# Expert stage: matmuls in program order, background work spread over the experts, a gather moved ahead of a branch

## The chip, the cores and the metric

One core of a Trainium2 chip runs the kernel. The time is device microseconds, the median of three runs. A profile of one further execution shows the engines: TensorE (PE, and PEld for its weight loads), VectorE (DVE), ScalarE (ACT), GpSimd (POOL) and SyncE (SP), which here issues the weight loads. Each engine works through its own queue in order and waits for others at semaphores.

## The reference, cut to what matters

Two transformer blocks on one sequence of 256 tokens, model width 1024, float32. The first block mixes by convolution and windowed attention and ends in a mixture of 32 experts. The second mixes by attention with an extra context and by a long ("Hyena") convolution, and ends in a PEER layer. The change lies in the experts of the first block:

```python
order = jnp.argsort(expert_id, stable=True)          # two experts per token
...
hmid = jax.nn.silu(xb @ w_gate[e]) * (xb @ w_up[e])  # 1024 -> 512
return (hmid @ w_down[e]) * wt[:, None]              # 512 -> 1024
...
out = jnp.zeros((t, d)).at[slot_token].add(ys)
h = h + hierarchical_moe(rms_norm(h, g_ffn[l]), ...)
```

Beside them the kernel computes things of the second block that don't depend on the first: keys and values of the context (`context_kv`) and the spectra of the two Hyena filters (`implicit_filters`: three sine layers, a fourth matmul, a decay, a division by the sum of absolute values, a Fourier transform).

## The kernel before, in words

Each expert gets 64 slots. `gather` (L957 on) builds, for four experts at a time, the one-hot selection on VectorE and multiplies it with the tokens on TensorE (L977, L978); the result `XT` holds the inputs of the four experts. Then per expert: `expert_up` multiplies with gate and up weights, the two in different halves of the array's columns, into one PSUM tile (L1013), and ScalarE copies it to `ex` (L1016); `expert_mid` transposes it (L1024) and forms the gated product `em` on ScalarE and VectorE (L1026 to L1029); `expert_down` multiplies with the down weights (L1041), again in two column halves, and ScalarE and VectorE scale by the slot's weight into `eyh`, `eyl` (L1047, L1048). Every two experts, `selw` transposes their selection weights (L995) and `combine` multiplies back to tokens (L1059) and adds to `h` (L1061). A float32 matmul shows as two instructions.

The weights come as tiles of 512 KB, eight for up and four for down per expert, on SyncE's queue (`wload`, L87), into a ring of 14 tiles. Sixteen more buffers serve once, at the stage's start, for experts 1 and 2 (`early`); `self.wrap` is set until they are used up, and until then no background runs, since it needs their space. A load waits until the tile's last reader is done.

The loop is `experts(lo, hi)` (L846 on). It traces down of the expert before behind up of this one. The background is a Python generator, `background` (L1064 on); each `yield` ends a step, there are 33, and `back()` runs one, twice per expert. The generator's own loads are issued by ScalarE.

The order of the trace isn't the order of issue. The framework's scheduler plans all engines with a cost model: among instructions that are ready it takes the one traced first, so it may set matmuls of other parts into a run where its model has the next weights late. `add_manual_dep` with NoSync fixes the order of two instructions on one engine, without a semaphore.

After 28 experts comes `overflow`, a block under a runtime condition (more than 64 tokens for some expert) on all engines; nothing crosses it. The first eight tiles of expert 28 (`pre`) are loaded ahead of it. It isn't taken with these inputs: no instruction of it is in the trace. Then `experts(28, 32, pre)` runs the last four.

Of the kernel before, what the change touches and what calls it, by code (L numbers as in the profile page):

```python
# [8 lines left out]
F32 = mybir.dt.float32  # L9
F32R = mybir.dt.float32r  # L10
# [3 lines left out]
AF = mybir.ActivationFunctionType  # L14
OP = mybir.AluOpType
# [4 lines left out]
D = 1024  # L20
# [24 lines left out]
class K:  # L45
# [693 lines left out]
    def moe(self):  # L739
# [105 lines left out]

        def experts(lo, hi, pre=None):  # L846
            def group(e):
                return self.gather(R[:, :, e:e + 4], W[:, :, e:e + 4])

            cur = group(lo)  # L850
            sws, mid, pend, y = [], None, None, None
            for e in range(lo, hi + 1):

                if e < hi:
                    if e % 4 == 0 and e > lo:
                        cur = nxt
# [15 lines left out]
                if e > lo and e % 2 == 0:  # L872
                    pend = y, sws.pop(0)
            self.combine(*pend)

        bg = None

        def back():
            nonlocal bg
            if not self.wrap:  # L880
                if not bg:
                    self.open_bp()
                    bg = self.background()
                next(bg, 0)

# [4 lines left out]
        self.wrap = pools  # L890
        experts(0, 28)
        for _ in bg:
# [11 lines left out]
        nc.vector.tensor_tensor(self.gf2, self.gf, self.gf, op=OP.mult)  # L904
        experts(28, 32, pre)

    def overflow(self, many, wg, wu, wd):
# [3 lines left out]
        with self.tc.If(many > 64):  # L911
# [12 lines left out]
            for j in range(7):  # L924
# [22 lines left out]
                e = nc.values_load(ei[0:1, 0:1], engines=[mybir.EngineType.SP], min_val=0, max_val=31)  # L947
                XT, sw = self.gather(rj, wj)

# [8 lines left out]

    def gather(self, R4, W4):
# [5 lines left out]
        sg = self.T(me, [128, 2, 4, 64], F32R, "selg", 2)[:, :, 0:n, :]  # L965
        tt(sg, self.iota[:, None, None, 0:64].to_broadcast(sh), R4[:, :, :, None].to_broadcast(sh), op=OP.is_equal)
        sw = self.T(me, [128, 2, 4, 64], F32, "selw", 2)[:, :, 0:n, :]
        tt(sw, sg.bitcast(F32), W4[:, :, :, None].to_broadcast(sh), op=OP.mult)
        XT = self.T(me, [128, 8, 256], F32, "XT", 2)[:, :, 0:64 * n]
# [12 lines left out]
        return XT, sw  # L982

# [48 lines left out]
    def expert_down(self, m, d, odd, sw, y=None):  # L1032
# [30 lines left out]

    def background(self):  # L1064
        nc, A, l1, hp = self.nc, self.A, self.l2, self.hp
        bp = self.bp
# [5 lines left out]
        for t in range(2):  # L1072
# [10 lines left out]
        yield  # L1083
        hc = []
        for k2 in range(4):
# [11 lines left out]
            yield  # L1097
        kc = self.T(bp, [128, 2, 128], F32, "sa", 1)
        for i in range(2):
# [8 lines left out]
            nc.scalar.activation(o, p[:, :S].rearrange("p (t c) -> p t c", t=2), AF.Copy)  # L1108
            yield
        sq = self.T(bp, [128, 2, 128], F32, "sn", 1)  # L1110
# [7 lines left out]
        tt(k4, k4, self.rv[:, None, o:o + 64].to_broadcast([128, 4, 64]), op=OP.mult)  # L1118
        yield
# [4 lines left out]
        yield  # L1124

# [6 lines left out]
        for i in range(3):  # L1132
# [13 lines left out]
            if i < 2:  # L1146
                w = wf[:, 64 * (i + 1):64 * (i + 2)]
            yield
        dec = self.T(bp, [128, 2, 512], F32, "dec")
# [7 lines left out]
        for o in range(2):  # L1157
            rsk = self.T(hp, [128, 2, 512], F32, "lo")
            rn, sk = rsk[:, 0], rsk[:, 1]
            nc.scalar.dma_start(sk, A["skip"][o:o + 1, :].to_broadcast([128, 512]))  # L1160
            pn = self.ps()
            fb = []
            w4 = self.T(hp, [64, 2, 512], F32, "hi")
            nc.scalar.dma_start(w4, A["hfw4"][:, 1024 * o:1024 * o + 1024].rearrange("p (a c) -> p a c", a=2))
            for dr in range(2):
                f = self.T(hp, [128, 2, 512], F32, "hi")
                for t in range(2):
                    p = self.ps()
                    nc.tensor.matmul(p, cur[:, t * 128:(t + 1) * 128], w4[:, dr, :], start=True, stop=True)
                    tt(f[:, t, :], p, dec[:, t, :], op=OP.mult)  # L1170
                    if dr == 1 and t == 0:

                        nc.vector.memset(f[0:1, 0, :], 0.0)
# [3 lines left out]
                    yield  # L1177
# [6 lines left out]
            tt(df, fb[0], fb[1], op=OP.subtract)  # L1184
            yield
            kf = [self.T(l1, [128, 2, 512], F32, "kf%s%d" % (c, o)) for c in "ab"]
            kf = [kf[i // 2][:, i % 2, :] if i < 4 else kfc[:, o] for i in range(5)]
            for i in range(5):
# [6 lines left out]
                if i not in (2, 3):  # L1195
                    tt(kf[i], kf[i], sk, op=OP.add)
                yield
            self.kf.append(kf)
# [931 lines left out]
```

## Time and profile before

| | |
|---|---|
| median of 3 runs | 1667.43 us (1666.98 to 1669.1) |
| the profiled execution | 1665.63 us |
| its span, first to last instruction | 1663.8 us |
| PE busy | 1573.6 us (95%) |
| DVE busy | 965.0 us (58%) |
| ACT busy | 495.3 us (30%) |
| moved by DMA | 536.53 MB |
| granted PE clock, mean | 0.981 |

The expert stage reaches from about 200 to 745 us of the span. A busy PE isn't a PE at its peak: the ends of matmuls are modelled, so short pauses between shapes don't show as idle. The distance from one start to the next tells more than a duration does. "Granted clock" is the share of 2.4 GHz that the chip let PE have.

### The profile page before, as it was taken

The numbers are of one execution on the slowest core, as the hardware profiler recorded it, in microseconds if no ns is written. First come the engines' busy times: TensorE is split into PE (matmuls) and PEld (weight loads), VectorE is DVE, ScalarE is ACT, GpSimd is POOL, SyncE is SP. The second block draws the span as 40 slices with busy tenths as digits, with TensorE's granted clock in tenths as the row PEclk, the third lists the DMA queues.
The fourth block names the chain that finished last, engine by engine and source line by source line (L and its number), as shares of the span: only waits on it lengthen the run. The fifth ranks groups of instructions, "written<-read, shape, count | busy, mean of one in ns | idle before, by whom it ended". The sixth has DMA issues, their size and how long they took to land. (4 is left out here: it accounts for less than half of the span.)

```text
span 1663.8 us, 25750 instructions
## 1 busy us (share of the span) xinstructions
PE 1573.6 (95%) x9884; PEld 1199.4 (72%) x9884; DVE 965.0 (58%) x2111; ACT 495.3 (30%) x1220; POOL 119.8 (7%) x122
## 2 busy tenths in 40 slices
PE   7999799999999999788999989899999999699996
PEld 7977644433333343337869889899999999699996
DVE  6987523334353322248988999866676766534443
ACT  5444322222211121126444444124444400000001
POOL 0000000000000000001000000111111112211121
PEclk9999899999999999999999999999999999799998
DMA  9548679999989999896567747899999999999992
GB/s 373 180 116 320 240 296 400 355 369 327 365 319 342 386 399 418 328 367 203 170 198 236 253 155 279 296 414 390 357 363 353 364 396 415 415 413 414 414 413 87
DMA packets 135325, 536.53 MB, mean 322 GB/s; under 512 B 16180, under 2 KB 17181, under 8 KB 122781
## 3 DMA queue, kind: packets, MB, share of 16 engines
q1 hardware_dynamic: 117184, 426.07, 68.6%
q0 software_dynamic: 13824, 100.67, 15.1%
q10 hardware_dynamic: 4188, 8.09, 1.4%
q8 instruction: 79, 1.29, 0.3%
q14 instruction: 50, 0.40, 0.1%
HBM read 532.57 MB, written 2.10 MB: 321 GB/s over the span
## 5 line engine op out<-in xcount | busy, mean ns | idle before, releaser
L1768 DVE SCALAR_TENSOR_TENSOR g<-g,xd 128x1024 f32<-128x1024 f32 x96 | 117.4, 1223 | 143.1 <-DMA g<-in_uv_dram,gi 143.1
L1013 PE MATMUL ps<-wB,XT 128*64 128x512 f32 x492 | 154.5, 599 | 0.0
L1740 POOL DMA_INDIRECT g<-in_uv_dram,gi x96 | 98.8, 1029 | 503.3 <-PE ps L1623 145.7
L132 PE MATMUL ps<-xh,hi 128*128 128x256 f32 x416 | 123.1, 297 | 1.4 <-ACT hi L97 1.4
L138 PE MATMUL ps<-xh,lo 128*128 128x256 f32 x416 | 117.6, 283 | 0.5 <-DVE lo L98 0.5
L137 PE MATMUL ps<-xl,hi 128*128 128x256 f32 x416 | 117.6, 283 | 0.3 <-DVE xl L305 0.3
L1769 ACT ACTIVATE ga<-ga 128x1 f32<-128x1 f32 x96 | 19.4, 203 | 318.9 <-DVE g L1768 318.8
L1027 DVE SCALAR_TENSOR_TENSOR eth<-eth,ps 128x256 f32<-128x256 f32 x32 | 13.4, 419 | 156.9 <-ACT eth L1026 156.8
L1048 DVE SCALAR_TENSOR_TENSOR eyl<-ps,slotw,eyh 64x512 fp32r<-64x512 f32 x64 | 47.8, 746 | 88.2 <-ACT eyh L1047 87.5
L1013 PEld LDWEIGHTS ps<-wB,XT 128*64 128x64 f32 x492 | 42.7, 137 | 69.0 <-issue 64.7
L1016 ACT ACTIVATE ex<-ps 128x512 f32<-128x512 f32 x32 | 19.1, 597 | 236.7 <-PE ps L1013 229.4
L97 ACT ACTIVATE hi<-wA 128x1024 fp32r<-128x1024 f32 x63 | 66.7, 1060 | 73.0 <-PE ps L137 30.9
L98 DVE TENSOR_TENSOR lo<-wA,hi 128x1024 fp32r<-128x1024 f32 x63 | 77.7, 1237 | 17.8 <-ACT hi L97 16.0
L1623 PE MATMUL ps<-B,wA 128*128 128x160 f32 x608 | 85.9, 300 | 0.0
L1013 PE MATMUL ps<-wA,XT 128*64 128x512 f32 x288 | 85.8, 599 | 0.0
L1615 PE MATMUL ps<-x,wA 128*128 128x160 f32 x608 | 85.7, 299 | 0.0
L132 PEld LDWEIGHTS ps<-xh,hi 128*128 128x128 f32 x416 | 79.5, 191 | 7.5 <-issue 4.6
L1623 PEld LDWEIGHTS ps<-B,wA 128*128 128x128 f32 x608 | 83.5, 190 | 0.0
L1615 PEld LDWEIGHTS ps<-x,wA 128*128 128x128 f32 x608 | 83.3, 190 | 0.0
L137 PEld LDWEIGHTS ps<-xl,hi 128*128 128x128 f32 x416 | 79.4, 191 | 3.8 <-issue 3.1
L1623 PE MATMUL ps<-B,xm 128*128 128x160 f32 x576 | 81.9, 304 | 0.0
L1615 PE MATMUL ps<-x,xm 128*128 128x160 f32 x576 | 81.4, 299 | 0.0
(529 smaller groups left out, 3493.4 us busy)
## 6 DMA issues: line engine op xcount, KB each, us to landing
wB<-in_w_gate_dram SPq DMA_DIRECT2D x70, 512.0 KB, 5.7
wB<-in_w_down_dram SPq DMA_DIRECT2D x63, 512.0 KB, 8.1
wB<-in_w_up_dram SPq DMA_DIRECT2D x53, 512.0 KB, 8.0
wA<-in_ws_dram SPq DMA_DIRECT2D x51, 512.0 KB, 5.5
wA<-in_ut_dram SPq DMA_DIRECT2D x38, 512.0 KB, 8.5
wA<-in_v_dram SPq DMA_DIRECT2D x38, 512.0 KB, 15.0
wA<-in_w_gate_dram SPq DMA_DIRECT2D x36, 512.0 KB, 8.2
wA<-in_w_up_dram SPq DMA_DIRECT2D x36, 512.0 KB, 7.2
```

What stands on the lines that cost most here:

```text
L97: ins = self.nc.scalar.activation(hi, w, AF.Copy)
L98: self.last_split = self.nc.vector.tensor_tensor(lo, w, hi.bitcast(F32), op=OP.subtract)
L132: ins = mm(ps, ah, bh, start=first, stop=False)
L137: mm(ps, ah, bl, start=False, stop=False)
L138: mm(ps, al, bh, start=False, stop=last)
L1013: nc.tensor.matmul(p[64 * s:64 * s + 64, :], XT[:, k, :], w[s][:, a, :], start=k == 0, stop=k == 7)
L1048: nc.vector.scalar_tensor_tensor(y[1][r, s, :], p[r, :], w, y[0][r, s, :].bitcast(F32), op0=OP.mult, op1=OP.subtract)
L1615: self.pace_pe = nc.tensor.matmul(p, w[:, k, :], x32[:, k, N0:], start=k == 0, stop=k == 7)
L1623: self.pace_pe = nc.tensor.matmul(acc[k][:, N0:], w[:, k * 128:(k + 1) * 128], B[:, c, :], start=c == 0, stop=c == 127)
L1740: ins = nc.gpsimd.indirect_dma_start(out=buf[i], out_offset=None, in_=A["uv"], in_offset=bass.IndirectOffsetOnAxis(ap=self.gi[:, i // J, i ...
L1768: stt(t, t, 1.0, self.gx[s], op0=OP.mult, op1=OP.mult, accum_out=a)
L1769: nc.scalar.activation(a, a, AF.Gelu_apprx_tanh)
```

## The change

- All PE instructions traced in `experts` are chained with NoSync dependencies in the order of the trace.
- That order is now: up of expert e, down of e-1, a background step, mid of e, combine of the pair before, selw, gather for the next four, perhaps a second background step.
- `back` counts steps: it returns while steps x 3 >= (e + 1) x 4, and it runs no second step in one expert when the step before yielded True, which marks results that the next step reads.
- The gather for expert 28 is made at expert 26, inside the first call, and handed to the second (`cur`). `overflow` gets tiles of its own for its gather.
- `expert_down` issues its halves in the order (odd, 1 - odd), so rows 0 to 63 of PSUM always come first.
- The sum of absolute values is formed by three additions on VectorE and one matmul with `ones` per filter; before it was four accumulating matmuls.

```diff
-        def experts(lo, hi, pre=None):
+        def experts(lo, hi, pre=None, cur=None):
...
-            cur = group(lo)
+            bb = nc.cur_bb
+            traced = len(bb.bb.instructions)
+            cur = nxt = cur or group(lo)
...
-                    if e % 2 == 0:
-                        sws.append(self.selw(cur[1], e % 4))
-                back()
-                if pend:
-                    self.combine(*pend)
-                    pend = None
                 if e > lo:
                     y = self.expert_down(mid, lambda j: wd[e - 1][:, j, :], (e - 1) % 2, sws[0],
                                          y if e % 2 == 0 else None)
                 if e < hi:
+                    back(e)
                     mid = self.expert_mid(st)
-                    if e % 4 == 2 and e + 2 < hi:
+                    if pend:
+                        self.combine(*pend)
+                        pend = None
+                    if e % 2 == 0:
+                        sws.append(self.selw(cur[1], e % 4))
+                    if e % 4 == 2 and e + 2 < 32:
                         nxt = group(e + 2)
-                back()
+                    back(e, True)
...
+            q = [i for i in bb.bb.instructions[traced:] if i.engine == mybir.EngineType.PE]
+            for i, j in zip(q, q[1:]):
+                self.tc.add_manual_dep(j, i.name, mybir.DependencyInfo(
+                    mybir.DependencyClass.NoSync, mybir.DependencyReason.DATA), reason="issue order")
+            return nxt
...
+        def back(e, again=False):
+            nonlocal bg, steps, fresh
+            if self.wrap or steps * 3 >= (e + 1) * 4 or again and fresh:
+                return
+            if not bg:
+                self.open_bp()
+                bg = self.background()
+            fresh = next(bg, True)
+            steps += 1
...
-        experts(0, 28)
+        cur = experts(0, 28)
...
-        experts(28, 32, pre)
+        experts(28, 32, pre, cur)
...
-            for s in range(2):
+            for s in (odd, 1 - odd):
                 r = 64 * (s ^ odd)
...
-                    ab = self.T(bp, [128, 512], F32, "ab", 1)
-                    nc.scalar.activation(ab, f[:, t, :], AF.Abs)
-                    nc.tensor.matmul(pn, ones, ab, start=dr == 0 and t == 0, stop=dr == 1 and t == 1)
-                    yield
+                    if dr == 0 and t == 0:
+                        nc.scalar.activation(ab, f[:, t, :], AF.Abs)
+                    else:
+                        aa = self.T(bp, [128, 512], F32, "aa", 1)
+                        nc.scalar.activation(aa, f[:, t, :], AF.Abs)
+                        tt(ab, ab, aa, op=OP.add)
+                    yield dr * t == 1
                 fb.append(f)
+            pn = self.ps()
+            nc.tensor.matmul(pn, ones, ab, start=True, stop=True)
```

## Rows read from the trace of the kernel before

**Rows 1.** The page's slices: busy tenths of PE, 41.6 us each.
```profile
PE   7999799999999999788999989899999999699996
```

**Rows 2.** Stretches: PE, PEld, DVE, ACT, POOL busy; clock, DMA share, GB/s.
```profile
250.00:540.00 290.00, 287.76 (x1210) 114.52 (x1208) 112.16 (x193) 67.49 (x123) 1.01 (x1) 1.00 0.95 354
560.00:660.00 100.00, 99.13 (x414) 36.91 (x412) 30.14 (x51) 18.79 (x34) 0.00 (x0) 1.00 1.02 411
250.00:680.00 430.00, 421.17 (x1766) 163.77 (x1764) 154.42 (x265) 93.31 (x169) 1.01 (x1) 1.00 0.96 369
```

**Rows 3.** Waits of SyncE's queue, 250 to 540 us: total, times, longest.
```profile
SPq L87 <- PE ps L1013: 117.8, 100, 4.5
SPq L87 <- PE ps L1041: 69.1, 57, 3.5
```

**Rows 4.** Timeline of ACT (start, us, instruction, idle before): copies of experts 3, 19, 27.
```profile
250.52 0.60 ACT L1016 ACTIVATE ex<-ps 128x512 f32<-128x512 f32 x1 [4.20 <-PE ps L1013]
...
544.70 0.60 ACT L1016 ACTIVATE ex<-ps 128x512 f32<-128x512 f32 x1 [10.53 <-PE ps L1013]
...
663.75 0.60 ACT L1016 ACTIVATE ex<-ps 128x512 f32<-128x512 f32 x1 [9.88 <-PE ps L1013]
```

**Rows 5.** Timeline of PE, 622 to 624 us: an up run broken.
```profile
622.48 1.02 PE L1013 MATMUL ps<-wB,XT 128*64 128x512 f32 x2
623.43 0.50 PE L1059 MATMUL ps<-eyh,selwT 128*128 128x512 f32 x1
624.21 0.50 PE L1059 MATMUL ps<-eyl,selwT 128*128 128x512 f32 x1 [0.28 <-DVE eyl L1048]
```

**Rows 6.** Timeline of PE, 239 to 265 us: unbroken runs.
```profile
239.29 0.36 PE L977 MATMUL ps<-selg,xnh 128*128 128x256 f32 x1
...
243.30 1.94 PE L1013 MATMUL ps<-wB,XT 128*64 128x512 f32 x8
...
250.32 0.51 PE L1059 MATMUL ps<-eyh,selwT 128*128 128x512 f32 x1
...
252.39 1.08 PE L1041 MATMUL ps<-wB,em 128*64 128x512 f32 x4
...
255.97 0.75 PE L1024 MATMUL ps<-ident,ex 128*128 128x128 f32 x4
256.55 0.60 PE L1092 MATMUL ps<-ident,hi 128*128 128x128 f32 x4
...
264.10 0.44 PE L995 MATMUL ps<-ident,selw 128*128 128x128 f32 x2
...
264.59 0.60 PE L1092 MATMUL ps<-ident,hi 128*128 128x128 f32 x4
```

**Rows 7.** Groups by line, PE, 250 to 545 us: busy, mean ns, idle before.
```profile
L1193 PE MATMUL ps<-lo,FK 128*128 128x512 f32 x40 | 19.3, 601 | 0.0
L1176 PE MATMUL ps<-ab,ones 128*128 128x512 f32 x16 | 9.0, 645 | 0.8 <-ACT ab L1175 0.8
L1169 PE MATMUL ps<-hi,sh 64*128 64x512 f32 x16 | 9.0, 641 | 1.2 <-ACT sh L1145 1.2
L1105 PE MATMUL ps<-hi,lo 128*128 128x128 f32 x64 | 8.1, 280 | 0.0
```

**Rows 8.** Timeline at the branch (675 to 690 us), and expert 0's mid (215.80).
```profile
215.80 0.75 PE L1024 MATMUL ps<-ident,ex 128*128 128x128 f32 x4 [0.72 <-ACT ex L1016]
...
674.87 0.72 PE L1059 MATMUL ps<-eyl,selwT 128*128 128x512 f32 x2
680.99 0.69 DVE L966 TENSOR_TENSOR selg<-iota,t 128x512 fp32r<-128x512 f32 x1 [4.30 <-PEq L911]
...
681.83 0.55 PE L977 MATMUL ps<-selg,xnh 128*128 128x256 f32 x1 [6.24 <-DVE selg L966]
...
687.97 1.94 PE L1013 MATMUL ps<-wB,XT 128*64 128x512 f32 x8
```

**Rows 9.** Stretches again: the first 5 us behind the branch.
```profile
680.00:685.00 5.00, 3.17 (x15) 3.20 (x16) 2.02 (x6) 0.84 (x2) 0.00 (x0) 0.50 0.49 132
```

More of the change, by code (lines that the diff above doesn't have):

```diff
@@ L867, in experts @@
                 if e < hi:
+                    back(e)
                     mid = self.expert_mid(st)
-                    if e % 4 == 2 and e + 2 < hi:
+                    if pend:
[4 more added lines that the diff above has]
+                    if e % 4 == 2 and e + 2 < 32:
                         nxt = group(e + 2)
-                back()
+                    back(e, True)
                 if e > lo and e % 2 == 0:
+                    if pend:
+                        self.combine(*pend)
                     pend = y, sws.pop(0)
             self.combine(*pend)
[L876 to L884, printed above, removed]
+            q = [i for i in bb.bb.instructions[traced:] if i.engine == mybir.EngineType.PE]
[3 more added lines that the diff above has]
+            return nxt
+        bg, steps, fresh = None, 0, False
+        def back(e, again=False):
[7 more added lines that the diff above has]
+            steps += 1
         pools = self.wpools
@@ L947, in overflow @@
                 e = nc.values_load(ei[0:1, 0:1], engines=[mybir.EngineType.SP], min_val=0, max_val=31)
-                XT, sw = self.gather(rj, wj)
+                t = self.T(self.hp, [128, D], F32, "lo")
+                XT, sw = self.gather(rj, wj, [self.T(self.hp, [128, 128], F32R, "lo"), t[:, 0:128], t[:, 512:D]])
                 def part(w, a, n):
@@ L957, in overflow, with gather @@
                 self.combine(y, sw, 1)
-    def gather(self, R4, W4):
+    def gather(self, R4, W4, own=None):
         nc, me = self.nc, self.me
@@ L964, in gather @@
         sh = [128, 2, n, 64]
-        sg = self.T(me, [128, 2, 4, 64], F32R, "selg", 2)[:, :, 0:n, :]
+        if own:
+            sg, sw = [x.rearrange("p (t e s) -> p t e s", t=2, e=n) for x in own[:2]]
+            XT = own[2].rearrange("p (k s) -> p k s", k=8)
+        else:
+            sg = self.T(me, [128, 2, 4, 64], F32R, "selg", 2)[:, :, 0:n, :]
+            sw = self.T(me, [128, 2, 4, 64], F32, "selw", 2)[:, :, 0:n, :]
+            XT = self.T(me, [128, 8, 256], F32, "XT", 2)[:, :, 0:64 * n]
         tt(sg, self.iota[:, None, None, 0:64].to_broadcast(sh), R4[:, :, :, None].to_broadcast(sh), op=OP.is_equal)
-        sw = self.T(me, [128, 2, 4, 64], F32, "selw", 2)[:, :, 0:n, :]
         tt(sw, sg.bitcast(F32), W4[:, :, :, None].to_broadcast(sh), op=OP.mult)
-        XT = self.T(me, [128, 8, 256], F32, "XT", 2)[:, :, 0:64 * n]
         for k2 in range(4):
@@ L1078, in background @@
             cx.append(c)
-        yield
+        yield True
         rs = self.rsqrt(bp, ss, 1.0 / D, [128, 2])
@@ L1082, in background @@
             ts(cx[t], cx[t], rs[:, t:t + 1], None, op0=OP.mult)
-        yield
+        yield True
         hc = []
@@ L1096, in background @@
                                      bias=self.modT[:, k, 1:2])
-            yield
+            yield k2 == 3
         kc = self.T(bp, [128, 2, 128], F32, "sa", 1)
@@ L1108, in background @@
             nc.scalar.activation(o, p[:, :S].rearrange("p (t c) -> p t c", t=2), AF.Copy)
-            yield
+            yield i == 1
         sq = self.T(bp, [128, 2, 128], F32, "sn", 1)
@@ L1118, in background @@
         tt(k4, k4, self.rv[:, None, o:o + 64].to_broadcast([128, 4, 64]), op=OP.mult)
-        yield
+        yield True
         p = self.ps()
@@ L1123, in background @@
         nc.scalar.activation(self.kT2[:, 256:512], p[:, :S], AF.Copy)
-        yield
+        yield False
         zT = self.T(bp, [33, S], F32, "zT")
@@ L1147, in background @@
                 w = wf[:, 64 * (i + 1):64 * (i + 2)]
-            yield
+            yield True
         dec = self.T(bp, [128, 2, 512], F32, "dec")
@@ L1160, in background @@
             nc.scalar.dma_start(sk, A["skip"][o:o + 1, :].to_broadcast([128, 512]))
-            pn = self.ps()
+            ab = self.T(bp, [128, 512], F32, "ab", 1)
             fb = []
@@ L1173, in background @@
                         nc.vector.memset(f[0:1, 0, :], 0.0)
-                    ab = self.T(bp, [128, 512], F32, "ab", 1)
-                    nc.scalar.activation(ab, f[:, t, :], AF.Abs)
-                    nc.tensor.matmul(pn, ones, ab, start=dr == 0 and t == 0, stop=dr == 1 and t == 1)
-                    yield
+                    if dr == 0 and t == 0:
+                        nc.scalar.activation(ab, f[:, t, :], AF.Abs)
+                    else:
+                        aa = self.T(bp, [128, 512], F32, "aa", 1)
+                        nc.scalar.activation(aa, f[:, t, :], AF.Abs)
+                        tt(ab, ab, aa, op=OP.add)
+                    yield dr * t == 1
                 fb.append(f)
+            pn = self.ps()
+            nc.tensor.matmul(pn, ones, ab, start=True, stop=True)
             ts(rn, pn, EPS, None, op0=OP.add)
@@ L1184, in background @@
             tt(df, fb[0], fb[1], op=OP.subtract)
-            yield
+            yield True
             kf = [self.T(l1, [128, 2, 512], F32, "kf%s%d" % (c, o)) for c in "ab"]
@@ L1196, in background @@
                     tt(kf[i], kf[i], sk, op=OP.add)
-                yield
+                yield False
             self.kf.append(kf)
```

## The prediction

> **What bounds the kernel now.** The page's slices first: tensor engine (PE) at nine tenths nearly everywhere, with a dent in the 17th slice [rows 1]. The change touches only the expert stage, so the next view is the busy time of stretches. In 250 to 540 us PE is busy 287.76 of 290 us while the loads run at 354 GB/s; in 560 to 660 they run at 411 GB/s [rows 2]. So the first half isn't held by memory, or the rate would be the same in both. The queue's own waits say what holds it: in 250 to 540 SyncE waited 117.8 us for up matmuls and 69.1 us for down matmuls to give a weight tile back [rows 3]. PE is the bound there; in 560 to 660 both are close. The difference is the background work (context K/V and Hyena filters of the second block): by the code two steps per expert from expert 2, all 33 gone by about expert 19. The copies of the up result (`ex`, one per expert) give the pace: 250.52 for expert 3, 544.70 for expert 19, 663.75 for expert 27 [rows 4]. That is 18.4 us per expert with background and 14.9 without.
>
> How much of 18.4 is work? The order of PE has holes that are not shown as idle: at 622.48 two up matmuls stand alone between other shapes and take 0.95 us to the next start [rows 5], where two in a long run take 0.44 (7.02 us for 32, below). The scheduler's order breaks up and down runs like this several times per expert.
>
> **The change, part by part.** Durations are those of the profiled execution: 1665.63 us in all, span 1663.8; the median shown is 1667.43, 1.8 above it.
>
> *Program order on PE.* Where the old order happens to be unbroken, from 243.30 to 264.59, start to start gives prices: up 7.02 (243.30 to 250.32), combine of a pair 2.07, down 3.58, mid 0.58, selw 0.49, gather 4.01 (239.29 to 243.30) [rows 6]. Four experts are 4 x (7.02 + 3.58 + 0.58) + 2 x (2.07 + 0.49) + 4.01 = 53.9 us, 13.5 each. From expert 3 to 27 there are six such fours, 323.1 us; the gather for expert 28, now traced at expert 26, is the sixth of their gathers. Down follows up directly, so in program order ex's round trip through ScalarE (ACT) is covered by 3.58 us of down; at expert 0, where nothing lay between, PE idled 0.72 us [rows 8]. The swapped half order in odd down projections keeps halves alternating from up into down; the 3.58 is that of an even one, so it costs nothing on top. In the old order it would have left one half pair uncovered, about 0.2 us in each of 14.
>
> *Background spread and lightened.* Its PE work, by lines: filter transforms 19.3 us, filter matmuls 9.0, K/V 8.1, sums of absolute values 9.0 [rows 7]. The last go from 16 instructions to 4, so 2.3. The 16 transposes are priced like mid's (0.58 per four, 2.3) and the ten small matmuls and transposes left at 1.2, an estimate. Sum 42 us. VectorE (DVE) gets six additions of 128x512; the nearest row of that size is 0.69 us [rows 8], 4.1 in all, hidden: DVE is busy 112.16 us of 290 [rows 2]; without that cover they would cost at most their 4.1. By the new rule (at most 4/3 steps per expert so far, no second step behind one whose results are fresh) I count the first step at expert 2 and the last at 24, never more than two in one expert. So PE needs 250.52 + 323.1 + 42 = 615.6 for expert 27's ex.
>
> *What is late next: the loads.* From 250 to 680 they moved 369 x 430 = 158.7 MB [rows 2], through expert 28's first eight tiles. At 411 GB/s that is 386 us, to 636; the last eight tiles (512 KB each) take 10.2 and expert 27's four down tiles 5.1 of it, so expert 27's up weights are there at 621. PE 616 and loads 621: with the work level, both bind nearly everywhere, and each will sometimes wait for the other. I allow 10 us for that, about half a ring of 14 tiles (14 x 1.28 = 18 us at this rate); both ends are 0 and 30. Expert 27's ex then comes at 631 instead of 663.75, 32.7 earlier. Behind it now stands also a combine (2.07) that the old order had ahead of it: 30.7 left.
>
> A rule of the Trainium skill stands against this part: "DMA: Bandwidth & Descriptors", Specifications, puts a core's share of memory bandwidth at about 358 GB/s. By that the 158.7 MB would need 443 us, more than the 430 they took, and this part would bring nothing. The trace disagrees: 411 GB/s over 100 us [rows 2].
>
> *Step loads and waits in PE's queue.* Program order makes PE wait behind a step whose operands are late. The step's loads sit on ACT's queue, which the order is not imposed on; they go out as soon as a tile is free, so I cost them at nothing; late, a 512 KB load would cost at least its own 1.28 us at 411 GB/s, at four steps. Behind a waiting step stand that expert's mid, then combine, then the next up, so the release of weight tiles and with it the loads. That is rival 1.
>
> *Gather ahead of the overflow branch.* PE's last combine ends at 675.59; the branch lets DVE go at 680.99, DVE makes the selection, PE gathers from 681.83 and starts expert 28's up matmuls at 687.97 [rows 8]. Now up needs only the first eight tiles, loaded meanwhile, and can start at about 681.0: 7.0 earlier. But the granted clock was 0.50 from 680 to 685 [rows 9], 1.2 of 2.4 GHz, after 6.24 us of idle, and the gather ran in it: 6.14 us (681.83 to 687.97) where it took 4.01 at full clock [rows 6]. Those 2.1 us now fall on up matmuls; the first ex round trip is uncovered as it was before. The loads, 132 GB/s in that window, restart as much earlier. That leaves 4.9; I take 4, between 0 (the loads take it all) and 7. The overflow block's own tiles lie in a branch that isn't taken; nothing.
>
> Sum: 30.7 + 4 = 34.7 us. 1665.63 - 34.7 = 1631, with 1.8 to the median 1633. Nothing behind the stage changes.
>
> **Rivals.**
> 1. *Slower: the head of PE's queue.* In each expert the mid and the background step wait for what ACT or DVE made in the same expert or the one before, and nothing may pass them. For: 0.28 us of idle at 624.21 [rows 5] and 0.72 at 215.80 [rows 8] happen wherever no other matmul stands between. Against: the flag on fresh results keeps each step an expert away from its operands, and PE's idle in 250 to 540 is 2.2 us in all. Priced at 0.72 for each of 24 mids and two such trips, 1.44, for each of 30 steps with PE work: 60 us, less the 10 allowed: 1683. It decides from 1.45 us per expert (34.7 / 24).
> 2. *The loads don't go faster.* If 369 GB/s is what the stream gives beside this mix, the stage's end stays and only the branch gains: 1663. For: the stretch with background ran at 354 [rows 2]. Against: the queue's waits are for PE [rows 3].
> 3. *Half of it.* Bursts without a tile's release (gather 4.01, combine 2.07, two transforms 3.6 in a row) and small waits of the first kind cost 27 us instead of 10: 1650.
> 4. *The work isn't levelled as I count it*: the background already ends by expert 19 again, and only the breaks go. Then 16 experts take 13.5 + 2.6 and the rest run at the loads' pace. 250.52 + 16 x 16.1 + 8 x 15.3 (512 KB x 12 at 411) = 630.5: the same number, for the reason that PE was the bound; a rival for the cause, not for the time.
>
> **How the numbers follow.** Forecast, rival 4 with it: 0.64, with its own range 1616 (no mutual waits and a branch worth 7 make 13, a load rate 1% over 411 another 4) to 1644. Rival 3: 0.18. Rival 2: 0.07. Rival 1: 0.11, of which a small part ends near no change. What a measurement of this kernel can tell from no change is about 0.2%, 3.3 us. Faster 0.87, the same 0.04 (between rivals 1 and 2), slower 0.09. The range takes forecast and rival 3: 1616 to 1656.
>
> **What would show it.** Right: ex copies 15.5 to 16 us apart from expert 3 to 27 with no step at 19; 400 GB/s or more from 260 to the branch; up as one run of 32 matmuls; up of expert 28 first behind the branch, at half clock; sum-of-absolutes matmuls down to four. Wrong: idle of PE before mid or background matmuls (rival 1), a full load queue at 370 GB/s (rival 2), the stage's end past 715 (it was 745).

## The result, and the profile after

The changed kernel takes 1625.16 us in the median of four runs (1621.56 to 1626.39), the kernel before on the same chip 1667.2 us (four runs, 1664.92 to 1669.1): ratio 0.9736, 95% interval 0.9711 to 0.9762. Predicted were 1633, between 1616 and 1656. The profiled span went from 1663.8 to 1623.6 us, 40.2 less.

The page's slices of the changed kernel, 40.6 us each: busy tenths of PE, and what the DMA engines moved.

```profile
PE   7999799999999997979999899999999999699996
GB/s 371 182 132 301 273 277 381 381 418 410 418 419 418 419 418 342 417 223 155 210 185 270 185 169 303 376 404 345 366 363 356 357 409 415 416 413 413 414 414 80
```

The expert stage is slices 6 to 18. PE looks as it did in [rows 1]; what is new stands in the second line, seven slices at 410 to 419 GB/s. The same in the view of stretches (busy time of PE, PEld, DVE, ACT, POOL with instruction counts; granted clock, DMA share, GB/s):

```profile
250.00:540.00 290.00, 285.77 (x1368) 125.50 (x1366) 120.61 (x218) 76.11 (x137) 1.01 (x1) 0.99 1.02 411
...
250.00:630.00 380.00, 372.23 (x1781) 164.44 (x1777) 149.90 (x270) 98.17 (x179) 1.01 (x1) 0.99 1.02 413
...
635.00:640.00 5.00, 3.51 (x10) 1.18 (x12) 0.63 (x4) 0.00 (x0) 0.00 (x0) 0.50 0.30 95
640.00:645.00 5.00, 5.00 (x20) 1.65 (x18) 1.22 (x1) 0.00 (x0) 0.00 (x0) 0.77 0.83 266
```

In 290 us PE now does 1368 matmul instructions where it did 1210 [rows 2], in slightly less busy time: "busy" had held the breaks. The load queue's waits in 250 to 540 us (total, times, longest) turned with it:

```profile
SPq L87 <- PE ps L1031: 39.4, 36, 6.1
SPq L87 <- DMA wB<-in_w_gate_dram: 31.0, 37, 2.7
```

Up matmuls hold tiles back for 39.4 us instead of 117.8 [rows 3]; behind them stand waits for the queue's own transfers. Memory and PE are both close to their limit. The pace, by ScalarE's copies for experts 3, 19 and 27 (start, duration; idle of ScalarE before):

```profile
249.91 0.60 ACT L1034 ACTIVATE ex<-ps 128x512 f32<-128x512 f32 x1 [4.46 <-PE ps L1031]
...
497.79 0.60 ACT L1034 ACTIVATE ex<-ps 128x512 f32<-128x512 f32 x1 [4.99 <-PE ps L1031]
...
615.16 0.60 ACT L1034 ACTIVATE ex<-ps 128x512 f32<-128x512 f32 x1 [6.27 <-PE ps L1031]
```

That is 15.5 us per expert up to expert 19 and 14.7 behind it, against 18.4 and 14.9 [rows 4]; the step is nearly gone. One expert on PE's timeline (start, duration of the run):

```profile
255.68 3.65 PE L1031 MATMUL ps<-wB,XT 128*64 128x512 f32 x16
259.17 3.60 PE L1031 MATMUL ps<-wA,XT 128*64 128x512 f32 x16
262.60 2.74 PE L1060 MATMUL ps<-wB,em 128*64 128x512 f32 x12
265.18 1.03 PE L1060 MATMUL ps<-wC,em 128*64 128x512 f32 x4
266.13 0.66 PE L1112 MATMUL ps<-ident,hi 128*128 128x128 f32 x4
```

Up takes 6.92 us in one run and down 3.53, as in the unbroken pieces of [rows 6]; nothing like [rows 5] is left. The background by groups, 250 to 640 us (busy, mean ns, idle before), answers to [rows 7], with the sums of absolute values down from 16 matmuls to 4:

```profile
L1218 PE MATMUL ps<-lo,FK 128*128 128x512 f32 x40 | 19.5, 610 | 0.0
...
L1203 PE MATMUL ps<-ab,ones 128*128 128x512 f32 x4 | 2.2, 644 | 0.0
```

Last, PE's timeline from expert 27's up matmuls to those of expert 28 behind the branch, which answers to [rows 8]; in brackets idle time and what ended it:

```profile
611.42 3.60 PE L1031 MATMUL ps<-wB,XT 128*64 128x512 f32 x16
614.86 3.60 PE L1060 MATMUL ps<-wA,em 128*64 128x512 f32 x16
...
622.24 2.80 PE L1060 MATMUL ps<-wB,em 128*64 128x512 f32 x12 [1.24 <-DVE em L1047]
...
626.68 0.49 PE L1078 MATMUL ps<-eyh,selwT 128*128 128x512 f32 x1 [0.78 <-ACT eyh L1066]
...
629.41 0.79 PE L1078 MATMUL ps<-eyl,selwT 128*128 128x512 f32 x1 [0.72 <-DVE eyl L1067]
...
631.28 0.63 PE L1078 MATMUL ps<-eyl,selwT 128*128 128x512 f32 x1
636.49 6.54 PE L1031 MATMUL ps<-wB,XT 128*64 128x512 f32 x16 [4.59 <-PEq L924]
```

From the end of the last combine to the first up matmul behind the branch it is now 4.58 us (631.91 to 636.49), before 12.38 (675.59 to 687.97). The first 16 up matmuls then take 6.54 us instead of 3.60, at granted clock 0.50 (1.2 of 2.4 GHz), as in [rows 9].

Where the 40.2 us of span are, before to after: until expert 3's ex 250.52 to 249.91 (-0.6); expert 3 to 27 413.23 to 365.25 (**-48.0**); from there to the last combine's end 11.84 to 16.75 (+4.9); the gap over the branch 12.38 to 4.58 (-7.8); the last four experts 57.59 to 63.63 (+6.0); on to the next stage's first matmul 5.95 to 5.57 (-0.4); everything behind, which the change does not touch, 912.3 to 918.0 (+5.6).

### The profile page after: what moved, and what is told of

Its sections match the earlier page's. It is cut to its first block, busy times and chain, and to the rows that moved or that the text cites. A ratio compares the mean times of both kernels' runs of the same rounds, so it can differ in the third digit from the quotient of the medians.

```text
span 1623.6 us, 25732 instructions
## 1 busy us (share of the span) xinstructions
PE 1527.8 (94%) x9872; PEld 1200.8 (74%) x9872; DVE 960.9 (59%) x2117; ACT 496.0 (31%) x1222; POOL 120.1 (7%) x122
## 3 DMA queue, kind: packets, MB, share of 16 engines
q0 software_dynamic: 13824, 100.67, 15.5%
## 5 line engine op out<-in xcount | busy, mean ns | idle before, releaser
L1031 PE MATMUL ps<-wB,XT 128*64 128x512 f32 x492 | 133.2, 609 | 4.7 <-PEq L924 4.6
L1067 DVE SCALAR_TENSOR_TENSOR eyl<-ps,slotw,eyh 64x512 fp32r<-64x512 f32 x64 | 47.6, 743 | 119.0 <-ACT eyh L1066 118.7
L1080 DVE TENSOR_TENSOR h<-h,ps 128x512 f32<-128x512 f32 x64 | 42.2, 682 | 70.3 <-PE ps L1078 70.3
L1779 DVE SCALAR_TENSOR_TENSOR xd<-g,gw,xd 128x1024 f32<-128x1024 f32 x62 | 79.7, 1285 | 2.1
L1648 PEld LDWEIGHTS ps<-B,xm 128*128 128x128 f32 x576 | 80.1, 193 | 0.0
```

What stands on the lines that cost most here:

```text
L1031: nc.tensor.matmul(p[64 * s:64 * s + 64, :], XT[:, k, :], w[s][:, a, :], start=k == 0, stop=k == 7)
L1067: nc.vector.scalar_tensor_tensor(y[1][r, s, :], p[r, :], w, y[0][r, s, :].bitcast(F32), op0=OP.mult, op1=OP.subtract)
L1648: self.pace_pe = nc.tensor.matmul(acc[k][:, N0:], w[:, k * 128:(k + 1) * 128], B[:, c, :], start=c == 0, stop=c == 127)
L1779: stt(acc, t, w, acc, op0=OP.mult, op1=OP.add)
```

## The experiments

All times are medians; the kernel before ran beside the experiments at 1668.8 to 1669.6 and beside the changed kernel at 1667.2, and each ratio is to the one beside it. For each profiled run the table splits the stretch from expert 3's to expert 27's ex: PE's idle time, what half clock cost (the sum over 5 us pieces of (1 - granted clock) x 5), and the rest: PE's work, with what pauses don't show as idle. The shape switches are counted from PE's records: how often a matmul has another tile shape (128\*64, 128\*128, ...) than the one before. Half clock that falls into idle time counts in both columns and makes the rest too small by as much: 3.2 us in e2, 1.0 in e9, nothing in the others of the table. The changed kernel was profiled twice (last two rows), so a difference of 2 us between two stretches says nothing.

| kernel | median (range, runs) | ratio, 95% | stretch | idle | half clock | rest | switches |
|---|---|---|---|---|---|---|---|
| before | 1668.8 to 1669.6 | 1 | 413.2 | 3.1 | 0.0 | 410.1 | 195 |
| e6, levelled pace alone | 1665.66 (1662.78-1671.49, 10) | 0.9979 [0.9965, 0.9992] | 410.9 | 1.4 | 0.0 | 409.6 | 194 |
| e12, chain alone | 1670.34 (1665.26-1673.65, 10) | 0.9997 [0.9985, 1.0010] | 402.6 | 17.5 | 10.2 | 374.9 | 113 |
| e9, program order alone | 1644.71 (1642.27-1647.14, 4) | 0.9857 [0.9838, 0.9877] | 385.4 | 5.7 | 5.1 | 374.6 | 106 |
| e5, after: no chain, old pace | 1631.34 (1630.26-1636.5, 4) | 0.9769 [0.9741, 0.9798] | 377.1 | 3.9 | 3.4 | 369.8 | 102 |
| e2, after: old pace | 1647.61 (1642.94-1651.68, 4) | 0.9850 [0.9822, 0.9878] | 388.9 | 19.2 | 8.5 | 361.1 | 59 |
| e1, after: no chain | 1619.6 (1618.11-1620.93, 4) | 0.9694 [0.9668, 0.9720] | 366.5 | 0.2 | 0.0 | 366.4 | 103 |
| after | 1625.16 (1621.56-1626.39, 4) | 0.9736 [0.9711, 0.9762] | 365.3 | 4.5 | 1.7 | 359.0 | 59 |
| e10, after once more | 1626.63 (1620.96-1626.9, 5) | 0.9732 [0.9712, 0.9752] | 363.3 | 4.5 | 0.0 | 358.9 | 59 |

"Program order" means here the order in which the kernel's code gives the instructions to the scheduler; the chain is the four lines that force PE into it.

**e1: the chain taken out, all else as changed.**

```diff
-            q = [i for i in bb.bb.instructions[traced:] if i.engine == mybir.EngineType.PE]
-            for i, j in zip(q, q[1:]):
-                self.tc.add_manual_dep(j, i.name, mybir.DependencyInfo(
-                    mybir.DependencyClass.NoSync, mybir.DependencyReason.DATA), reason="issue order")
```

> The changed kernel without the chain on the tensor engine: levelled background and the early gather stay, the scheduler orders the matmuls again. Theory A (the breaks in the matmul runs were the larger loss): an expert costs 14.9 us as in the old stretch without background, plus 42/24 = 1.75 of background, 16.6 in all against 15.2 now, so 24 x 1.4 = 34 us are lost: 1655 to 1660. Theory B (the bunched background was the loss, the order hardly counts): at most 8 us lost, 1625 to 1633.

Measured 1619.6: without the chain the gain is whole, and by the median 5.6 us larger, though the two intervals overlap a little. It lies below theory B's range as well. PE's timeline of one expert in this kernel shows why:

```profile
459.09 1.89 PE L1027 MATMUL ps<-wB,XT 128*64 128x512 f32 x8
460.81 3.60 PE L1027 MATMUL ps<-wA,XT 128*64 128x512 f32 x16
464.24 1.89 PE L1027 MATMUL ps<-wB,XT 128*64 128x512 f32 x8
465.95 1.03 PE L1056 MATMUL ps<-wB,em 128*64 128x512 f32 x4
```

The scheduler left to itself gives whole up runs too. It still splits down by a step, mid and a combine (the other twelve of its matmuls stand at 470.51; 103 switches instead of 59), but next to up it sets down, which has the same tile shape. So the chain isn't what mends the order, and theory A, which gave it the gain, falls; theory B's reason falls with e6.

**e2: the chain and the new program order, with the old pace of two steps per expert.**

```diff
-            if self.wrap or steps * 3 >= (e + 1) * 4 or again and fresh:
+            if self.wrap:
```

> The changed kernel with the old pace of the background, two steps in each expert from expert 2 whether results are fresh or not; the chain and the early gather stay. Theory A with rival 4 of the prediction (16 experts at 13.5 + 2.6, 8 at the loads' 15.05, and no waits): ex of expert 27 at 628 instead of 615, so 1635 to 1640. Theory B: most of the gain goes, 1650 or more. Rival 1 of the prediction (the head of the queue waits): steps now stand right behind the step that makes their operands, some ten times; at 1.4 us each another 14 us, 1650, with idle of the tensor engine before background matmuls to be seen.

Measured 1647.61: between A's range and the rival's 1650, and with the rival's idle time. PE's waits in 250 to 660 us (total, times, longest):

```profile
PE ps L1189 <- ACT sh L1165: 6.6, 1, 6.6
PE ps L1154 <- ACT sh L1165: 5.5, 1, 5.5
PE ps L1203 <- DVE ab L1199: 5.1, 2, 2.8
```

This is the prediction's rival 1: filter steps run before their operands are there, and behind the chain nothing may pass. Idle 19.2 and half clock 8.5 us. With the chain the pace is worth 23.6 us (388.9 - 365.3), and 18.3 of it (19.2 + 8.5 - 3.2 - 4.5 - 1.7) is waiting and its clock.

**e3: expert 28's gather behind the branch again.**

```diff
-                    if e % 4 == 2 and e + 2 < 32:
+                    if e % 4 == 2 and e + 2 < hi:
...
-        experts(28, 32, pre, cur)
+        experts(28, 32, pre)
```

> The changed kernel with the gather for expert 28 made behind the branch again. Theory: the early gather is worth 7.8 us at the branch, less some 3 for up matmuls at half clock: 1628 to 1631. Rival: behind the branch the loads are the bound, and the gather costs nothing there while it frees 4 us of matmul time at expert 26: 1625 or a little less.

Measured 1628.1 (1619.93 to 1629.16, six runs; ratio 0.9731 [0.9706, 0.9756]). From expert 27's ex to 28's it takes 35.0 us against 31.4 in the changed kernel, so the part does save 3.6 us there. But the stretch before is 361.5 instead of 365.3 (363.3 in the repeat), 2 to 4 less, and the stage ends at 705.08, against 705.69 and 704.14: the gather's 4 us of matmuls seem to be paid on one side of the branch or on the other. In the total 1628.1 and 1625.16 (1626.63 in the repeat) are too close to tell apart.

**e4: the short tail.** The last expert ahead of the branch runs up, combine, mid, then the two downs.

```diff
+                last = e == hi - 1
+                if last:
+                    self.combine(*pend)
+                    pend, new = None, self.expert_mid(st)
...
-                    mid = self.expert_mid(st)
+                    mid = new if last else self.expert_mid(st)
```

> The changed kernel with another order in the last expert of each call (27 and 31): up, combine of the pair before, mid, down of the expert before, down of this one. In the profile of the changed kernel the stretch from the last ex copy to the last combine is 16.8 us at expert 27 and 17.5 at expert 31 (11.8 before the change at both): the combine stands between mid and down, em waits behind its additions on the vector engine (1.24 us of idle), and the clock falls in the pauses. Theory: about 4 us are gained at each, part of the first lost again to loads that aren't there yet: 1617 to 1621. Rival: the loads bind on both sides of the branch, and nothing is gained at the first: 1621 to 1623.

Measured 1619.61 (1617.65 to 1627.47, six runs; 0.9698 [0.9673, 0.9722]): the median is as expected, the cause is shown in part only. Expert 27's ex to 28's takes 28.7 us instead of 31.4, for the wait for `em` at 622.24 is gone, and expert 31's ex to the last combine 14.4 instead of 17.5. But the profiled execution (1626.7, 7 us over the median) ends the stage only 1.2 us earlier, at 704.46; the stretch up to expert 27 and the last experts are longer there.

**e5: neither chain nor levelled pace**: the edits of e1 and e2 together, so that the new program order and the small parts (half order, sums on VectorE, gather) stay.

> The changed kernel without the chain and with the old pace of two background steps per expert: what is left of the change is the order of the trace, the early gather and the small parts. Theory C (the order of the trace keeps the scheduler from breaking the runs, the chain adds nothing to it): an expert with background costs 13.5 + 2.8 + some 0.3, ex of expert 27 at about 633 and the kernel at 1634 to 1640, a little under the 1648 of the chained kernel at this pace, whose matmuls waited 17 us. Theory D (levelling is all): 18.4 us per expert with background as before, 1655 to 1663.

Measured 1631.34, a little below C's range and far from D's. Most of the gain is there without either.

**e6: the kernel before, with the levelled pace alone.**

```diff
-        def back():
+        def back(e):
...
+            if self.wrap or steps * 3 >= (e + 1) * 4:
+                return
...
+            steps += 1
```

> The kernel before with one part of the change: the background at no more than 4/3 steps per expert so far. Order of the trace, scheduler, gather, sums of absolute values stay as before. Theory D (levelling is all): as the changed kernel without the chain, less the branch's part: 1622 to 1630. Theory C (two halves, levelling and unbroken runs): 14.9 + 1.75 us per expert, ex of expert 27 near 650: 1650 to 1656.

Measured 1665.66: theory D falls, and C's size for this kernel was 10 us too low. Levelling alone moved background from early experts to late ones and left every break in place, as PE's timeline of this kernel shows:

```profile
467.41 1.02 PE L1017 MATMUL ps<-wA,XT 128*64 128x512 f32 x2
468.36 0.44 PE L999 MATMUL ps<-ident,selw 128*128 128x128 f32 x2
468.64 0.38 PE L999 MATMUL ps<-ident,sel 128*128 128x128 f32 x2
468.86 1.88 PE L1197 MATMUL ps<-lo,FK 128*128 128x512 f32 x4
470.67 3.22 PE L1017 MATMUL ps<-wA,XT 128*64 128x512 f32 x13
```

Two up instructions stand before `selw` and a background step, and take 0.95 us to the next start, as in [rows 5]. PE's total work stays (409.6), it is still the bound, and so it doesn't matter where the background lies.

**e7 and e8: which of the two limits holds the changed kernel?** e7 gives the down projections of five experts gate tiles that are already there instead of loads of their own; e8 multiplies by the high halves alone in gather and combine.

```diff
-            w = self.wload(d(j), [1024])
+            w = self.upw[j].rearrange("p a b -> p (a b)") if again else self.wload(d(j), [1024])
...
+            self.upw = (self.upw if kq else []) + [w[0]]
```
```diff
-                    nc.tensor.matmul(p[:, a, :], self.xnh[:, t, d], r, start=t == 0, stop=False)
-                    nc.tensor.matmul(p[:, a, :], self.xnl[:, t, d], r, start=False, stop=t == 1)
+                    nc.tensor.matmul(p[:, a, :], self.xnh[:, t, d], r, start=t == 0, stop=t == 1)
...
-                for i in range(2):
-                    nc.tensor.matmul(p, sw[0][r, s, t * 128:(t + 1) * 128], y[i][r, s, :], start=i == 0, stop=i == 1)
+                nc.tensor.matmul(p, sw[0][r, s, t * 128:(t + 1) * 128], y[0][r, s, :], start=True, stop=True)
```

> The changed kernel, in which the down projections of experts 7, 11, 15, 19 and 23 read the gate tiles of the next expert and load nothing: 20 of 384 loads left out, 25 us at 1.254 us each, all between the ex copies of experts 3 and 27; the output is not the reference's. Theory L (the loads alone bind there): the stretch falls from 365 to 340 us. Theory LP (loads and matmuls bind alike, the sum of the matmul prices being 365 too): it falls by 0 to 8 us.

> The changed kernel without the low halves in combine and gather: 24 us of matmuls left out between the ex copies of experts 3 and 27 (12 combines at 1.04, six gathers at 2.0); loads unchanged; the output is less exact. Theory L (the loads alone bind): the stretch stays within 3 us of 365. Theory LP: it falls by 0 to 8 us. If matmuls alone bind, it falls to 341.

e7: 1614.64 (two runs, 0.9661 [0.9633, 0.9690]), stretch 358.2, 7.1 shorter (5.2 against the repeat) for 25 us of transfers less. e8: 1619.38 (two runs, 0.9690 [0.9662, 0.9718]), stretch 364.4, between the changed kernel and its repeat, for 24 us of matmuls less. The queue's largest wait of e7 in 250 to 540 us, and PE's second-largest of e8 in 250 to 660 us:

```profile
SPq L87 <- PE ps L1032: 111.9, 66, 6.0
```
```profile
PE ps L1059 <- DMA wA<-in_w_down_dram: 5.0, 8, 1.7
```

e8 fits both theories, e7 only that of two limits close together. With fewer loads the queue waits for PE as it did before the change; with fewer matmuls PE waits for loads. The loads hold the stretch first, and PE lies 5 to 7 us behind them. That is why 59 switches or 103 make hardly any difference to it (e1). In e8 most of the 24 us doesn't even show as idle: the rest falls by 5.2 us, to 353.8, idle rises by 4.4. Where loads hold PE, "busy" contains waits too: by the starts in the trace 223 up and down instructions of e8 run without a partner in the other column half, 42 in the changed kernel and none in e7 (what that costs stands below).

**e9: the kernel before, with the new program order alone.** Down, a step, mid, combine, `selw`, gather, a step; no chain, no levelling, none of the small parts.

```diff
-                    if e % 2 == 0:
-                        sws.append(self.selw(cur[1], e % 4))
-                back()
-                if pend:
-                    self.combine(*pend)
-                    pend = None
...
+                    back()
                     mid = self.expert_mid(st)
+                    if pend:
+                        self.combine(*pend)
+                        pend = None
+                    if e % 2 == 0:
+                        sws.append(self.selw(cur[1], e % 4))
...
```

> The kernel before with one part of the change: the order of the trace inside an expert (down right behind up, background behind it, then mid, combine, selw, gather). No chain, old pace, gather behind the branch, four matmuls for each sum of absolute values. Theory C (this order keeps the runs whole): some 100 changes of tile shape instead of 195 between the ex copies of experts 3 and 27, the stretch at 380 to 386 us, the kernel at 1634 to 1642. Theory E (the small parts together with the order make it): 1650 or more.

Measured 1644.71: C's stretch (385.4), its total 3 us over. This one move takes 27.8 of the 48.0 us, and the switches from 195 to 106. e5 differs from it by the small parts together (half order, sums on VectorE, early gather): 8.3 us of stretch and 13.4 of the total; no run parts them.

**e10: the changed kernel once more, beside e11 and e12.**

> The changed kernel once more, on the chip of this call, to set the chain's cost against it: 1622 to 1627, so 3 to 8 us over the same kernel without the chain.

Measured 1626.63 (1620.96 to 1626.9, five runs; 0.9732 [0.9712, 0.9752]): the same kernel again.

**e11: e1 and e4 together.**

> The changed kernel without the chain and with the tail's order of experts 27 and 31. Theory: the scheduler already puts the mid of the last expert into the down run ahead of it (31.4 us from the ex copy of expert 27 to that of 28 with the chain, 28.2 without, 28.7 with the chain and the tail's order), so the two edits mend the same place: 1617 to 1622, as each alone. Rival: they mend different places: 1612 to 1615.

Measured 1623.79 (1619.28 to 1625.72, five runs; 0.9724 [0.9703, 0.9745]). The two edits don't add up; it is even slightly above the theory's 1622. Both kernels, e1 and e4, beat the changed one in the median; their intervals overlap with this one's, and which of the three is best these runs can't tell.

**e12: the kernel before, with the chain alone**, by the two lines shown and the four that e1 takes out.

```diff
+            bb = nc.cur_bb
+            traced = len(bb.bb.instructions)
```

> The kernel before with the chain alone: matmuls in the old order of the trace, old pace. Theory C' (unbroken runs are what counts, whoever keeps them): four changes of shape per expert at most, some 110 in the stretch, less the waits that the old pace costs a chained queue (17 us there): stretch 388 to 400, kernel at 1645 to 1657. Theory F (the chain by itself only adds waits): 1670 or more.

Measured 1670.34, no gain, at the edge of F; but F's reason is only half of it, for the breaks do go: 113 switches, rest 374.9 instead of 410.1, stretch 402.6, a little over the range of C'. Of these 35.2 us 24.6 are paid back in idle (+14.4) and half clock (+10.2). PE's largest wait of 250 to 660 us, and two places of it on the timeline, in the same kernel:

```profile
PE ps L1182 <- ACT ab L1181: 16.1, 8, 3.0
```
```profile
340.62 1.12 PE L1175 MATMUL ps<-hi,sh 64*128 64x512 f32 x2
343.19 2.06 PE L1182 MATMUL ps<-ab,ones 128*128 128x512 f32 x2 [1.44 <-ACT ab L1181]
...
352.00 1.12 PE L1175 MATMUL ps<-hi,sh 64*128 64x512 f32 x2
355.70 1.13 PE L1182 MATMUL ps<-ab,ones 128*128 128x512 f32 x2 [2.59 <-ACT ab L1181]
356.76 3.60 PE L1019 MATMUL ps<-wB,XT 128*64 128x512 f32 x8
```

In forced order each of eight steps with a sum of absolute values stops PE until ScalarE has made its operand, and slow matmuls follow: eight up matmuls take 3.60 us at 356.76, where [rows 6] have 1.94. The change has other means against those waits (three additions, one matmul, the flag on fresh results), and its idle time is 4.5 us. So these small parts seem to be what makes the chain bearable; no run takes them one by one. In the profiled execution, the longest of the ten (1673.65), the stage ends 3.5 us earlier than before (748.04 against 751.51), and what stands behind is 11.5 longer (below).

## Why the prediction was right, and where its steps were not

**What bounds the kernel: right.** PE, by breaks that the view counts as busy. e6, e9 and e12 show it apart from all else. Divided by the switches that went, it is 0.43 us each in e12, (410.1 - 374.9) / (195 - 113), and about as much in e9. But that is all that goes with a switch, not the price of the switch itself. Where nothing but the shape changes, as behind the down run at 265.18 in the fence of one expert, four instructions take 0.95 us to the next start, and twelve of the same run 2.58: 0.09 more than four have in a run. The Trainium skill has a rule for it: "TensorEngine Tiling (Array Packing)", Key Properties, says that changing the tiling mode drains the engine. The 0.09 us fit it; that they are the drain and nothing else, no run shows.

The 0.51 of [rows 5] (0.95 - 0.44) is mostly something else. The prediction's "two up matmuls" there are the two instructions of one float32 matmul. In a long run of the kernel before two instructions start together, by the code one for each half of the array's columns; in the broken one they run one after the other. Instructions of L1013 in 0.4 us of either ([rows 6], [rows 5]; us, PE busy with count; clock, DMA share, GB/s):

```profile
243.32:243.72 0.40, 0.40 (x2) 1.00 0.00 0
622.50:622.90 0.40, 0.40 (x1) 1.00 1.03 399
```

By the starts in the trace (a pair starts within 0.06 us), 127 of 1155 up and down instructions of the stretch have no partner in the kernel before, 66 in e12 and 71 in e9. At 0.215 us each (half of the 0.43 that a pair takes) that makes 13 of e12's 35 us, and the switches at 0.09 make 7. Another 2 are a combine that lies behind expert 27's ex there; what makes up the other 13 was not taken apart. So the half of the array that a broken run leaves empty costs more than the switch.

**Which part does it: wrong.** The prediction put the whole of it under "program order on PE" and took the chain for the means. By itself the chain gains nothing (e12); the place of combine, `selw` and the steps behind down does (e9), because the scheduler takes what was given to it first, and in the kernel before `selw`, a step and a combine stood between up and down. Combine and `selw` have another tile shape than up; down has the same, and keeps the halves in pairs (3.53 us for down in the fence of one expert).

**PE's sum, 615.6 for expert 27's ex: 615.16, but not for this reason.** The stretch is held by the loads (e8), so the hit doesn't test the sum. e7 does, for there the queue waits for PE: 358.2 us, where the sum had 365.1 (323.1 + 42), 7 too many.

**The loads, 621: mis-sized by one term.** From 250 to 630 us they ran at 413 GB/s, so the choice of the trace's 411 against the 358 of "DMA: Bandwidth & Descriptors" in the Trainium skill was right: that page's share is not what bound this core. But behind expert 27's up tiles the queue issues 16 tiles, not the 12 that were counted: the four of down(26) come first, because down of expert e-1 is given behind up of e. SyncE's timeline in the changed kernel shows the eight down tiles between expert 27's last up tile and expert 28's first:

```profile
602.00 0.33 SPq L87 DMA_DIRECT2D wB<-in_w_up_dram  x1
603.24 4.11 SPq L87 DMA_DIRECT2D wA<-in_w_down_dram  x4
608.24 2.76 SPq L87 DMA_DIRECT2D wB<-in_w_down_dram  x3
611.91 0.33 SPq L87 DMA_DIRECT2D wC<-in_w_down_dram  x1
613.33 0.33 SPq L87 DMA_DIRECT2D wB<-in_w_gate_dram  x1
```

Four tiles of 1.28 us are 5.1 us, and 621 becomes 616.

**Mutual waits, 10 us: about nothing.** With 616 for the loads, the measured 615.16 leaves none: PE, by e7 5 to 7 us quicker than they are, and a ring of 14 tiles between the two seem to have been enough. This and the 5.1 make 15.1 of the 15.3 us by which -32.7 fell short of -48.0. It is the step that failed in size. In the span the forecast missed by 5.5 us (40.2 instead of 34.7) and not by 15 because the tails and the stretch behind the stage erred the other way. That is luck; another 2 us lie between the profiled execution and the median.

**Tail, +2.07: +4.9 at expert 27, and +5.6 at expert 31, which was not counted.** The combine costs its 2.07, but it also puts three of its four additions of `h` into VectorE's queue ahead of `em`, so down(27) waits 1.24 us (622.24). After the pauses at `eyh` and `eyl` the clock is at half: the last combine matmuls take 0.63 us instead of 0.40. e4 takes the 1.24 out. At the end of the second call the order is the same. From expert 31's ex to the last combine's end it takes 17.5 us instead of 11.8, before and then after the change:

```profile
733.73 0.60 ACT L1016 ACTIVATE ex<-ps 128x512 f32<-128x512 f32 x1 [9.89 <-PE ps L1013]
744.84 0.73 PE L1059 MATMUL ps<-eyl,selwT 128*128 128x512 f32 x2
```
```profile
682.64 0.60 ACT L1034 ACTIVATE ex<-ps 128x512 f32<-128x512 f32 x1 [8.77 <-PE ps L1031]
699.49 0.63 PE L1078 MATMUL ps<-eyl,selwT 128*128 128x512 f32 x1
```

**Branch, -4: -7.8, of which 1.8 are given back.** The gap shrank as predicted (7.0) and the half clock was there. It cost more than the 2.1 us, 2.9 in the first 16 matmuls (6.54 - 3.60); up to expert 28's ex 1.8 remain of it (10.1 us instead of 8.3). The 6.0 us by which the last four experts came out longer are this 1.8, 1.5 less up to expert 31's ex, and the 5.6 of the second tail. e3, which undoes this part, ends the stage at the same time: it was worth nothing that could be measured.

**Nothing behind the stage changes: wrong, +5.6.** Code and work there are the same. In fourteen profiles that stretch varied from 912.3 to 923.8 us. Taken apart as in the table, but with half clock counted under busy PE alone, the rest is 856.8 to 858.9 in all fourteen, while idle varies from 44.9 to 53.8 and half clock from 7.2 to 15.3. From before to after the rest goes from 858.9 to 858.1, idle from 46.2 to 47.6, half clock from 7.2 to 12.3: the +5.6 is nearly all half clock, in several places. The clearest of them is one: PE's transposes of `x` in the PEER layer, first in the changed kernel, then in the kernel before (timeline of PE):

```profile
1051.98 0.69 PE L1925 MATMUL ps<-ident,x 128*128 128x128 f32 x2 [2.41 <-DVE x L1918]
1052.46 3.77 PE L1640 MATMUL ps<-x,wA 128*128 128x160 f32 x16
```
```profile
1094.64 0.44 PE L1900 MATMUL ps<-ident,x 128*128 128x128 f32 x2 [1.72 <-DVE x L1893]
1094.91 6.69 PE L1615 MATMUL ps<-x,wA 128*128 128x160 f32 x48
```

After 2.41 us of pause the clock was at half (16 matmuls in 3.77 us, where 48 take 6.69), after 1.72 it stayed. The length alone doesn't decide it: at 1053.79 in the kernel before it stayed after a pause of 2.38. Eight of the fourteen profiles have a half-clock piece at this place, and their stretch behind the stage is 920.3 us in the mean; the six without it (before and e1 among them) have 915.0. Of the +5.6 this place makes 2.2: 0.7 of pause and 1.5 of slow matmuls. What makes VectorE late there in one kernel and not in the other was not tested and stays open. As this stretch varies by several us from profile to profile, medians of e1, e3, e4, e11 and the changed kernel that lie 3 to 8 us apart don't rank them.

**Rivals.** 1 (1683): not in this change, but real, in e2 and e12; e2 shows that the levelled pace with its flag keeps it off, and the lighter sums may do so too. 2 (1663): fell, the loads went to 413. 3 (1650): fell. 4 (not levelled): the work was levelled. With the chain the old pace would not have given the same number (e2, 1647.61); without it expert 27's ex comes at 626.91 (e5), near this rival's 630.5.

## What to carry to other kernels

A matmul queue that is "busy" can still be losing time, at changes of tile shape and still more where a broken run leaves one half of the array without work: compare the distance from one start to the next, and look at what the code gives to the scheduler between two runs of one shape. Move that work behind them before you force an order, since a forced order turns every late operand into idle time for all that stands behind it, and often into a slow clock afterwards. When the bound moves to the loads, count the tiles in the order in which the queue issues them.

## What the runs showed of the hardware

A clean switch of tile shape cost 0.09 us (0.95 - 4 x 0.215, at 265.18 of the changed kernel). A half-array matmul instruction without a partner in the other half took the 0.43 us to the next start that two take together (622.48 against 243.30 in the kernel before). Neither shows as idle. The loads held 413 GB/s over 380 us beside a PE busy for 372 of them.

Short pauses of PE were followed by half clock in some cases and not in others. In e12 eight pauses, 1.4 to 3.0 us at the sum matmuls, with 17.5 us of idle in all, stood beside 10.2 us lost to it; in e9 it was 5.1 beside 5.7. In the changed kernel a pause of 1.40 us at 292.7 was followed by it and cost 1.7 us; in the repeat one of the same length at the same place was not.
